# A hybrid decoder layer: four column groups for the sums of squares of q and k, and other orders at the ends of the feed-forwards

## The chip, the cores and the metric

The kernel runs on one core of one Trainium2 chip. The metric is the device time of one execution in microseconds (us), and less is better. Given are the median of three runs and one more execution that the hardware profiler recorded.

The engines are TensorE (PE; its weight loads are listed as PEld), VectorE (DVE), ScalarE (ACT), GpSimd (POOL) and SyncE (SP). Each works through its own instructions in a fixed order and stops at the first one whose operands are not there. SP, ACT and POOL also start DMA transfers, as instructions in that same order.

## What is computed

One layer of a decoder for 1024 prompt tokens and 8 sample tokens, so T = 1032 columns, with D = 1024 channels and FF = 2816:

```python
h = h + 0.5 * swiglu(rmsnorm(h, g1), w_gu1, w_down1)
u = rmsnorm(h, g) @ w_in           # q | k | v (512 each) | conv value, gate | pool input (256 each)
A = dilated_attention(qknorm(q), qknorm(k), v)      # 8 heads of 64
B = conv_module(glu(value, gate))  # depthwise conv, layernorm, swish, pointwise
C = causal_pooling(pool_input)
h = h + concat(A, B, C) @ w_out
h = h + 0.5 * swiglu(rmsnorm(h, g2), w_gu2, w_down2)
def swiglu(x, w_gu, w_down):
    g, u = split(x @ w_gu, 2)
    return (silu(g) * u) @ w_down
```

The new keys, values, conv and pool states are outputs too. All in float32.

## The kernel before, in words

Activations lie with channels on the 128 partitions and tokens in the free direction. The 1032 columns are two halves `HF` of 516, each two quarters of QT = 258; the mixer cuts them into three pieces `CH` of CW = 344. A float32 matrix product is done as three matmuls of high and low parts (hi\*hi, hi\*lo, lo\*hi): `hi` copies the high part on ACT (L241), `lo` subtracts it on DVE or POOL (L244).

The program's five stages are: feed-forward 1 (`up` and `down` with n = 1; up to about 700 us), the mixer with the input projection, attention, conv and pooling (to about 1080 us), `out_proj` (to about 1176 us), feed-forward 2 (`up` and `down` with n = 2).

**`up`** computes the gate and up products of 22 inner tiles f with a seven-product Strassen scheme. `product(f, i, ...)` is 24 matmuls of 128x258 (L512 to L514) into one of four double PSUM banks. Products 1 and 2 of a tile use the same bank, one after the other: ACT copies the first out (`v`, L521), then product 2 goes on in that bank. The first tiles do their products 1 and 2 early (`kept`, L522), while the norm of the input is still being made. `lag` sets by how many tiles product 2 is behind product 1 in the list `order` (L600 to L612): 1 in feed-forward 1, 3 in feed-forward 2 (L887). After the early ones each tile runs products 5, 7, 4, 3 of itself and 1, 2, 6 of a later one. Products 6, 7 and 4 of a tile go through one bank, one after the other, and product 4 waits until DVE has added product 7's state of it into `v` (L565).

The norm of feed-forward 1 (`norms`, L393 to L418): x is fetched (`fetch_x`, L380 to L383, DMA on POOL's queue), ACT squares it (L405), DVE adds up the eight squares of a half (L407), and `total` has PE sum over the partitions (L388), ACT take the root (`sd`, L390) and DVE the reciprocal (L391). It is done first for half 0, whose x are in place already, and then for half 1 (`x_287`, `x_289`, `x_291`, `x_293`, `x_339`, `x_341`, `x_343`, `x_345`). The weights `wr` come through SP's queue; `wop` are their high and low parts. Afterwards `mixed` (L420 to L460) normalizes x and makes the operands of the other products.

**`down`** (L763 to L815) runs seven passes over 11 inner tiles, the last being pass 3; at the end of a pass `add` (L777) puts the bank into `h` and `store` writes it out.

**The mixer** (L952 to L1185): for each of four pairs (q tile, k tile) and three pieces, ACT copies the projection out and squares it (`sq`), and a `total` (L1116 to L1119) sums the squares of the head channels with 32-column weights `sel` into `acc`, q into partitions 0 to 31 and k into 32 to 63. Then v is projected in groups of 24 matmuls of 128x256 (L1158 to L1160), each followed by a two-record matmul `mat,r` (L1164). Beside them, `side_v` (L1187 to L1225) makes the norm factors: for each piece DVE multiplies `acc` twice by r (L1198, L1199), ACT takes the root (L1200, with an activation table load first), DVE the reciprocal (L1201) and a product (L1202), then the high part goes to `rr` on ACT and the low part on DVE (L244). `norm(t)` (L1217) has PE spread `rr` over the partitions. `next(tail)` steps through `conv_tail`, the layernorm of the conv module: `sh` and `sl` (high on ACT, low on POOL) of the conv output `cy`, their mean over the channels by PE (L277, `ones`), its subtraction on DVE (L1305), then squares in the same way.

**`out_proj`** (L897 to L950) adds its 16 pieces into the residual, stores each to `hd2` (L934, POOL's queue) and squares it on ACT (L935). POOL adds up the squares for feed-forward 2.

A scheduler with a timeline of its own orders the instructions of each engine ahead of time, from the order and the priorities of the code; the engines then keep that order. So an edit in one place may also move other instructions.

## Time and profile before

| what | value |
|---|---|
| median of three runs | 1855.25 us (1853.35, 1855.25, 1856.14) |
| the profiled execution | 1856.26 us, of which its span is 1854.5 us |
| granted clock of PE over the span | 0.996 of full speed |
| busy in the span | PE 1822.7 us (98%), PEld 94%, DVE 72%, ACT 39%, POOL 12% |
| chain of work that ended last | PE 90%, DVE 4%, DMA 3%, ACT 2% |

PE works nearly all the time, so the time is PE's work plus the places where PE waits or runs at the lower clock. Those places are found in the view of PE's waits, and then looked at in the timeline. "[0.45 <-ACT v L521]" behind a row means that the engine was idle for 0.45 us and that ACT's instruction of line 521 on tile `v` released it.

### The profile page before, as it was taken

To read this page: it belongs to the slowest core of one execution; us is meant where nothing else is said; L and a number is where in the kernel's file an instruction comes from. 1 tells how busy PE (TensorE), PEld (TensorE's weight loads), DVE (VectorE), ACT (ScalarE), POOL (GpSimd) and SP (SyncE) were. 2 spreads that over 40 slices of the span, in tenths; PEclk is the share of its full clock that TensorE was granted. 3 is DMA by queue.
4 is the path that set the end of the run, shared out by engine and by line. 5 is a ranking of instruction groups with operands and counts; after the bars stand their busy time and mean duration, and the time that the engine had idled before them with its cause. 6 is when DMAs were issued, how large, how long until landed. Compare 5 with 4: busy or idle time off the path is not lost.

```text
span 1854.5 us, 35895 instructions
## 1 busy us (share of the span) xinstructions
PE 1822.7 (98%) x14436; PEld 1750.0 (94%) x14436; DVE 1343.4 (72%) x2140; ACT 724.7 (39%) x1307; POOL 213.4 (12%) x205
## 2 busy tenths in 40 slices
PE   7999999999999999999899999999999999999999
PEld 7999999999999999998865689989999999999999
DVE  6877787778686566997666755577777877868654
ACT  6532222322333455235655653443222222243342
POOL 2100000000000004732532423200000000000000
PEclk9999999999999999999999999999999999999999
DMA  9544365454964243212353256654433435596421
GB/s 330 195 139 149 115 182 191 144 183 161 327 244 118 84 158 94 53 38 75 121 159 115 93 170 207 216 169 158 131 127 111 142 120 181 168 325 245 117 81 46
DMA packets 155578, 286.72 MB, mean 155 GB/s; under 512 B 25992, under 2 KB 32732, under 8 KB 155412
## 3 DMA queue, kind: packets, MB, share of 16 engines
q1 hardware_dynamic: 116276, 206.21, 35.7%
q10 hardware_dynamic: 34560, 63.20, 9.1%
q0 software_dynamic: 4576, 15.01, 2.4%
q8 instruction: 113, 1.85, 0.4%
q14 instruction: 53, 0.43, 0.1%
HBM read 208.29 MB, written 78.61 MB: 155 GB/s over the span
## 4 chain that ended last, share of the span: by engine, by line
PE 90%; DVE 4%; DMA 3%; ACT 2%; issue 1%; SPq 0%; ACTq 0%; DVEq 0%
PE ps L512 15%; PE ps L513 15%; PE ps L514 15%; PE ps L773 8%; PE ps L774 8%; PE ps L775 8%; PE ps L283 5%; PE ps L284 5%; PE ps L285 5%; PE ps L1599 2%; PE ps L1580 1%; DMA wr<-wgu 1%; PE ps L1527 1%; DVE pt L1530 1%; PE ps L1528 1%; PE ps L1159 1%
## 5 line engine op out<-in xcount | busy, mean ns | idle before, releaser
L512 PE MATMUL ps<-xot,wop 128*128 128x258 f32 x1408 | 396.3, 283 | 1.8 <-DVE v L565 1.8
L513 PE MATMUL ps<-xot,wop 128*128 128x258 f32 x1408 | 397.9, 283 | 0.0
L514 PE MATMUL ps<-xot,wop 128*128 128x258 f32 x1408 | 397.0, 282 | 0.0
L773 PE MATMUL ps<-mop,wop 128*128 128x258 f32 x1232 | 348.1, 283 | 0.9 <-DVE v L578 0.9
L774 PE MATMUL ps<-mop,wop 128*128 128x258 f32 x1232 | 347.4, 282 | 0.0
L775 PE MATMUL ps<-mop,wop 128*128 128x258 f32 x1232 | 346.6, 282 | 0.0
L512 PE MATMUL ps<-xo,wop 128*128 128x258 f32 x1056 | 301.3, 286 | 6.1 <-ACT v L521 3.9
L513 PE MATMUL ps<-xo,wop 128*128 128x258 f32 x1056 | 300.0, 284 | 0.0
L514 PE MATMUL ps<-xo,wop 128*128 128x258 f32 x1056 | 299.6, 284 | 0.4 <-DVE wop L244 0.4
L512 PEld LDWEIGHTS ps<-xot,wop 128*128 128x128 f32 x1408 | 265.1, 189 | 2.9 <-issue 2.6
L513 PEld LDWEIGHTS ps<-xot,wop 128*128 128x128 f32 x1408 | 265.8, 189 | 1.5 <-issue 1.5
L514 PEld LDWEIGHTS ps<-xot,wop 128*128 128x128 f32 x1408 | 265.9, 189 | 0.0
L774 PEld LDWEIGHTS ps<-mop,wop 128*128 128x128 f32 x1232 | 233.5, 190 | 0.0
L773 PEld LDWEIGHTS ps<-mop,wop 128*128 128x128 f32 x1232 | 232.2, 189 | 1.1 <-issue 1.1
L775 PEld LDWEIGHTS ps<-mop,wop 128*128 128x128 f32 x1232 | 232.7, 189 | 0.0
L241 ACT ACTIVATE wop<-s 128x512 fp32r<-128x512 f32 x176 | 105.8, 628 | 292.6 <-DVE s L478 227.9
L512 PEld LDWEIGHTS ps<-xo,wop 128*128 128x128 f32 x1056 | 201.1, 191 | 9.0 <-ACT v L521 5.5
L514 PEld LDWEIGHTS ps<-xo,wop 128*128 128x128 f32 x1056 | 201.2, 191 | 0.9 <-DVE wop L244 0.8
L513 PEld LDWEIGHTS ps<-xo,wop 128*128 128x128 f32 x1056 | 201.4, 191 | 0.3 <-DVE xo L374 0.2
L244 DVE TENSOR_TENSOR wop<-wr,wop 128x512 fp32r<-128x512 f32 x180 | 121.7, 696 | 55.1 <-ACT wop L241 54.9
L244 DVE TENSOR_TENSOR wop<-s,wop 128x512 fp32r<-128x512 f32 x176 | 117.7, 688 | 36.1 <-ACT wop L241 35.6
L241 ACT ACTIVATE wop<-wr 128x512 fp32r<-128x512 f32 x180 | 107.2, 622 | 89.1 <-PE ps L775 76.7
(263 smaller groups left out, 3404.8 us busy)
## 6 DMA issues: line engine op xcount, KB each, us to landing
wr<-wgu SPq DMA_DIRECT2D x227, 256.0 KB
mt<-v ACTq DMA_DIRECT2D x88, 258.0 KB
mr<-mt SPq DMA_DIRECT2D x88, 258.0 KB
m<-v ACTq DMA_DIRECT2D x66, 258.0 KB
mr<-m SPq DMA_DIRECT2D x66, 258.0 KB
kept<-v ACTq DMA_DIRECT2D x52, 258.0 KB
v<-kept SPq DMA_DIRECT2D x52, 258.0 KB
h<-hd SPq DMA_DIRECT2D x48, 258.0 KB
```

The lines of the kernel that those rows point to most:

```text
L241: self.nc.scalar.activation(out, src, AF.Copy)
L244: (eng or self.nc.vector).tensor_tensor(out, src, hi.bitcast(F32), op=ALU.subtract)
L283: mm(out, wh, xh, start=i == 0, stop=False)
L284: mm(out, wh, xl, start=False, stop=False)
L285: mm(out, wl, xh, start=False, stop=i == n - 1)
L512: mm(out, wh, xh, start=start and k == 0, stop=False)
L513: mm(out, wh, xl, start=False, stop=False)
L514: mm(out, wl, xh, start=False, stop=stop and k == HK - 1)
L773: mm(out, wh, mh, start=opens, stop=False)
L774: mm(out, wh, ml, start=False, stop=False)
L775: mm(out, wl, mh, start=False, stop=closes)
L1599: mm(O[half[e], q1 - w:q1], vt[j // 2][:, j % 2, hc:hc + 64], pT[:, e, :], start=j == 0, stop=j == 2 * b + 1)
```

## The change

- `fetch_x` takes a queue, and the eight x of half 1 that `norms` fetches go through SP's queue instead of POOL's; those of `mixed` stay on POOL's.
- In the last inner tile of `up` product 7 comes ahead of product 5; the addition of product 5's bank (`add_c`) is then done after product 5.
- In pass 2 of `down` the four banks are taken at once; with n = 1 in the order 3, 0, 1, 2.
- In pass 3 of `down` the last of the four column pieces is done in two halves, each with its own addition (`add_half`).
- Feed-forward 2 gets lag 2 instead of 3.
- `out_proj` stores to `hd2` through ACT's queue instead of POOL's.
- The eight additions of `xs` (the sample tokens' x, 128x8 each) go from POOL to DVE.
- The sums of squares: a piece of 344 columns is cut into two of CH2 = 172, and `total` writes four groups of 32 partitions (q and k of the left, q and k of the right columns) with four matmuls of 172 columns instead of two of 344. Roots and reciprocals then take 128 partitions x 172 columns instead of 64 x 344; the products with r go by 64 partitions. The high part is first made in a tile `stath` and copied into `rr` in two parts.
- Between the factors and the first `norm`, `conv_tail` is advanced four times instead of two.

```diff
-        def fetch_x(k, hf):
+        def fetch_x(k, hf, queue=nc.gpsimd):
             x = tmp(f"x{hf}")
-            nc.gpsimd.dma_start(x, src(k, hf))
+            queue.dma_start(x, src(k, hf))
             return x
...
-            xs = [fetch_x(k, 1) for k in range(HK)]
+            xs = [fetch_x(k, 1, nc.sync) for k in range(HK)]
...
-                            xs += [fetch_x(i, 1) for i in range(HK, KT)]
+                            xs += [fetch_x(i, 1, nc.sync) for i in range(HK, KT)]
...
             val[f, "c"] = product(f, 5, "c", True, False)
+            if (f, 7) in val:
+                add_c(f)
...
-            nc.vector.tensor_tensor(two(v), two(v), val[f, "c"], op=ALU.add)
+            if (f, "c") in val:
+                add_c(f)
+
+        def add_c(f):
+            v = two(val[f, 7])
+            nc.vector.tensor_tensor(v, v, val[f, "c"], op=ALU.add)
...
-            order += [(5, f), (7, f)]
+            order += [(5, f), (7, f)] if i + 1 < NF else [(7, f), (5, f)]
...
-            if opens:
+            if opens and p == 2 and j == 0:
+                for b in (3, 0, 1, 2) if n == 1 else range(4):
+                    bank[b] = self.psp.tile([P, 2, 512], F32, tag="ps", name="ps")
+            elif opens and p != 2:
                 bank[j] = self.psp.tile([P, 2, 512], F32, tag="ps", name="ps")
...
-            for q in range(2):
+            for q in qs:
...
+        def add_half(j, q):
+            x = h[j][:, HT + q * QT:HT + (q + 1) * QT]
+            nc.vector.scalar_tensor_tensor(x, bank[j][:, q, 0:QT], 0.5, x, op0=ALU.mult, op1=ALU.add)
...
+                    if (p, j, b[-1]) == (3, 3, NP - 1):
+                        for q in range(2):
+                            for i in b:
+                                product(p, i, j, (q,))
+                            add_half(j, q)
+                        store(j, 1, h[j][:, HF[1]])
+                        continue
...
-                gen = self.up(lambda k, hf: hd2[k][:, HF[hf]], 2, "g2", False, 3)
+                gen = self.up(lambda k, hf: hd2[k][:, HF[hf]], 2, "g2", False, 2)
...
-            nc.gpsimd.dma_start(hd2[d][:, HF[hf]], x)
+            nc.scalar.dma_start(hd2[d][:, HF[hf]], x)
...
-                    for e in range(2):
-                        nc.tensor.matmul(acc[c][32 * e:32 * e + 32], sel[:, 32 * p:32 * p + 32], parts[e],
-                                         start=p == 0, stop=p == 3)
+                    for g in range(4):
+                        nc.tensor.matmul(acc[c][32 * g:32 * g + 32], sel[:, 32 * p:32 * p + 32],
+                                         parts[g % 2][:, g // 2 * CH2:(g // 2 + 1) * CH2],
+                                         start=p == 0, stop=p == 3, skip_group_check=True)
...
         for c in range(3):
-            r = self.r[0:64, CH[c]]
-            nc.vector.tensor_tensor(sc[c], acc[c][0:64], r, op=ALU.mult)
-            nc.vector.tensor_tensor(sc[c], sc[c], r, op=ALU.mult)
-            nc.scalar.activation(sc[c], sc[c], AF.Sqrt, bias=self.eps[0:64])
-            nc.vector.reciprocal(sc[c], sc[c])
-            nc.vector.tensor_tensor(sc[c], sc[c], r, op=ALU.mult)
+            x = sc[c][:, 0:CH2]
+            for h in range(2):
+                nc.vector.tensor_tensor(x[half[h]], acc[c][half[h]], self.r[half[h], cols(c, h)], op=ALU.mult)
+                nc.vector.tensor_tensor(x[half[h]], x[half[h]], self.r[half[h], cols(c, h)], op=ALU.mult)
+            nc.scalar.activation(x, x, AF.Sqrt, bias=self.eps)
+            nc.vector.reciprocal(x, x)
+            for h in range(2):
+                nc.vector.tensor_tensor(x[half[h]], x[half[h]], self.r[half[h], cols(c, h)], op=ALU.mult)
...
         for c in range(3):
-            self.hi(rr[0:64, CH[c]], sc[c])
-            self.lo(rr[64:128, CH[c]], sc[c], rr[0:64, CH[c]])
-        next(tail, None)
-        yield
-        next(tail, None)
-        yield
+            x, xh = sc[c][:, 0:CH2], self.t("stath", dt=F32R)[:, 0:CH2]
+            self.hi(xh, x)
+            for h in range(2):
+                nc.scalar.activation(rr[0:64, cols(c, h)], xh[half[h]].bitcast(F32), AF.Copy)
+                self.lo(rr[64:128, cols(c, h)], x[half[h]], xh[half[h]])
+        for _ in range(4):
+            next(tail, None)
+            yield
```

Three places show how the instructions stand. First ACT at the start of feed-forward 1. Before, from the table load for the root of half 0 to the root of half 1:

```order
L390 ACT_TABLE_LOAD
L390 ACTIVATE sd<-ps,eps 128x516
L241 ACTIVATE wop<-wr 128x512 x2
L522 DMA kept_3_161<-v_501 128x516
L405 ACTIVATE x_343<-x_343 128x516
L521 ACTIVATE v_539<-ps 128x516
L241 ACTIVATE wop<-wr 128x512
L405 ACTIVATE x_345<-x_345 128x516
L522 DMA kept_2_160<-v_539 128x516
L241 ACTIVATE wop<-wr 128x512
L390 ACTIVATE sd<-ps,eps 128x516
```

The same place on ACT after the change, from the copy of the sixth product to the root of half 0:

```order
L522 ACTIVATE v_501<-ps 128x516
L406 ACTIVATE x_345<-x_345 128x516
L523 DMA kept_0_158<-v_388 128x516
L242 ACTIVATE wop<-wr 128x512
L523 DMA kept_2_160<-v_428 128x516
L391 ACT_TABLE_LOAD
L391 ACTIVATE sd<-ps,eps 128x516
```

The last square of half 1 (`x_345`) stood behind the table load and the first root and now stands ahead of both. On DVE, in the same way, the sum that ends half 1 now stands ahead of the first reciprocal.

Second, ACT while v is projected. Before, from the first high part for the conv mean:

```order
L241 ACTIVATE sh_10176<-cy0_8947 128x344
L1165 ACTIVATE misc_8362<-ps_10114 128x1
L1200 ACT_TABLE_LOAD
L1200 ACTIVATE stat_10118<-stat_10118,eps_65 64x344
L241 ACTIVATE sh_10180<-cy1_9462 128x344
L1166 ACTIVATE v0_10030<-ps_10083,misc_8362 128x256
L241 ACTIVATE wboth_10138<-wr_10136 128x512
L1200 ACTIVATE stat_10119<-stat_10119,eps_65 64x344
L241 ACTIVATE sh_10213<-cy0_8947 128x344
```

After, from the first root to that same high part (`sh_10222`):

```order
L1229 ACTIVATE stat_10143<-stat_10143,eps_65 128x172
L1229 ACTIVATE stat_10144<-stat_10144,eps_65 128x172
L1229 ACTIVATE stat_10145<-stat_10145,eps_65 128x172
L1188 ACTIVATE misc_8363<-ps_10200 128x1
L1189 ACTIVATE v0_10049<-ps_10175,misc_8363 128x256
L1188 ACTIVATE misc_8363<-ps_10255 128x1
L1189 ACTIVATE v1_10050<-ps_10230,misc_8363 128x256
L242 ACTIVATE stath_10204<-stat_10143 128x172
L1240 ACTIVATE rr_10072<-stath_10204 64x172 x2
L242 ACTIVATE stath_10210<-stat_10144 128x172
L242 ACTIVATE stath_10216<-stat_10145 128x172
L242 ACTIVATE sh_10222<-cy0_8948 128x344
```

All six `sh` of the conv mean stood ahead of the second high part of the factors or among the roots; now the first stands behind the high parts of all three pieces, and the other five follow it. On PE the first matmul that reads `sh` comes after the third `mat,r` of the v groups in both; the first `norm` came after four v groups and comes after six now.

Third, PE among the early products of feed-forward 2. Before, where product 2 of a tile takes over the bank of product 1 (`ps_13945`):

```order
L512 MATMUL ps_13945<-xo11_13061,wop_13714 128x258
L513 MATMUL ps_13945<-xo11_13061,wop_13714 128x258
L514 MATMUL ps_13945<-xo11_13061,wop_13714 128x258
L513 MATMUL ps_13868<-xo21_13568,wop_13904 128x258
L514 MATMUL ps_13868<-xo21_13568,wop_13904 128x258
L512 MATMUL ps_13945<-xo21_13568,wop_13981 128x258
```

After, where product 1 of one tile ends and product 2 of an earlier tile begins:

```order
L513 MATMUL ps_14030<-xo11_13107,wop_13799 128x258
L514 MATMUL ps_14030<-xo11_13107,wop_13799 128x258
L515 MATMUL ps_14030<-xo11_13107,wop_13799 128x258
L513 MATMUL ps_13878<-xo21_13610,wop_13838 128x258
L514 MATMUL ps_13878<-xo21_13610,wop_13838 128x258
L515 MATMUL ps_13878<-xo21_13610,wop_13838 128x258
```

Before, two matmuls lay between the end of product 1 in a bank and the start of product 2 in it; now whole products of 24 matmuls lie between.

## Rows read from the trace of the kernel before

**Rows 1.** The view of waits of PE over the whole span: tile and line of the instruction that waited, what released it, us in total, how many times, the longest.

```profile
PE ps L388 <- DVE x L407: 5.7, 1, 5.7
PE ps L1217 <- DVE rr L244: 5.5, 3, 4.0
PE ps L512 <- ACT v L521: 3.9, 8, 0.7
PE ps L512 <- ACT wop L241: 2.2, 2, 1.3
PE ps L512 <- DVE v L565: 1.8, 2, 0.9
PE ps L388 <- ACT x L405: 1.5, 1, 1.5
PE ps L284 <- DVE xl L296: 1.3, 1, 1.3
```

**Rows 2.** The timeline of PE around the two totals of the norm in feed-forward 1: start in us, duration, engine, line, operation, names and shapes, count, idle time before it and what released it. Lines 388 are the totals, of half 0 and of half 1.

```profile
28.98 1.11 PE L388 MATMUL ps<-sq,mat 128*128 128x258 f32 x4 [1.49 <-ACT x L405]
29.74 0.47 PE L512 MATMUL ps<-xo,wop 128*128 128x258 f32 x1
35.56 0.28 PE L514 MATMUL ps<-xo,wop 128*128 128x258 f32 x1
41.58 2.06 PE L388 MATMUL ps<-x,mat 128*128 128x258 f32 x4 [5.74 <-DVE x L407]
43.08 0.78 PE L512 MATMUL ps<-xo,wop 128*128 128x258 f32 x1
47.16 0.28 PE L512 MATMUL ps<-xo,wop 128*128 128x258 f32 x1
```

**Rows 3.** The same stretch on ACT, DVE and POOL (timeline, as in rows 2): the last square of half 1, the reciprocal of half 0, the eighth fetch of x; from the view of DMA issues from 0 to 45 us the line of these fetches (count, KB each, median us from issue to landing); and from the view by stretches one of 2 us (length, then busy us and count on PE, PEld, DVE, ACT, POOL; granted clock of PE; DMA share; GB/s).

```profile
36.93 0.63 ACT L405 ACTIVATE x<-x 128x516 f32<-128x516 f32 x1
...
34.50 3.38 DVE L391 RECIPROCAL r<-sd 128x516 f32<-128x516 f32 x1 [1.23 <-ACT sd L390]
...
19.57 0.54 POOL L382 DMA_DIRECT2D x<-x  x1 [9.20 <-DVE sq L407]
...
x<-x POOLq DMA_DIRECT2D x15, 258.0 KB, 5.5
...
42.00:44.00 2.00, 2.00 (x7) 1.63 (x7) 0.00 (x0) 0.32 (x1) 0.33 (x2) 0.50 0.88 285
```

**Rows 4.** The timeline of PE at two of the eight waits among the early products of feed-forward 2.

```profile
1204.58 0.39 PE L512 MATMUL ps<-xo,wop 128*128 128x258 f32 x1 [0.45 <-ACT v L521]
...
1211.08 0.39 PE L512 MATMUL ps<-xo,wop 128*128 128x258 f32 x1 [0.45 <-ACT v L521]
```

**Rows 5.** The timeline of PE at the end of `up` and the start of `down` in feed-forward 1, and of DVE at the kernel's end.

```profile
463.97 0.36 PE L512 MATMUL ps<-xot,wop 128*128 128x258 f32 x1 [0.88 <-DVE v L565]
470.86 0.36 PE L773 MATMUL ps<-mop,wop 128*128 128x258 f32 x1 [0.88 <-DVE v L578]
...
1850.51 0.70 DVE L785 SCALAR_TENSOR_TENSOR h<-ps,h 128x516 f32<-128x516 f32 x1 [0.76 <-PE ps L775]
```

**Rows 6.** The chain of work that ended last, at the last store of `out_proj` (start, us, what), and the timeline of PE at the wait behind it.

```profile
1176.37 5.96 DMA hd<-h
...
1186.07 0.39 PE L512 MATMUL ps<-xo,wop 128*128 128x258 f32 x1 [0.94 <-ACT wop L241]
```

**Rows 7.** The timeline of PE and of its weight loads: one total of the sums of squares (L1118, two column groups) with the matmul after it, and the products of the sample tokens (L1075, four column groups of 32 partitions).

```profile
789.47 0.77 PE L1118 MATMUL ps<-sq,sel 128*32 128x344 f32 x4
790.17 0.43 PE L283 MATMUL ps<-xh,whi 128*128 128x344 f32 x1
...
865.73 1.05 PE L1075 MATMUL ps<-wr,xs 128*8 128x256 f32 x16
...
865.73 0.55 PEld L1075 LDWEIGHTS ps<-wr,xs 128*8 128x8 f32 x16 [0.21 <-issue]
```

**Rows 8.** The timeline of PE from the first conv mean (L277) past the first two norms (L1217); L1158 is a matmul of the v projection.

```profile
878.59 0.42 PE L277 MATMUL ps<-sh,ones 128*128 128x344 f32 x1
...
882.26 0.38 PE L1164 MATMUL ps<-mat,r 1*128 1x1 f32 x2
886.62 0.66 PE L1217 MATMUL ps<-rr,bcx 128*128 128x344 f32 x1 [3.98 <-DVE rr L244]
...
891.07 0.41 PE L1158 MATMUL ps<-whi,xh 128*128 128x256 f32 x1
893.56 0.28 PE L1158 MATMUL ps<-whi,xh 128*128 128x256 f32 x1
...
895.37 0.74 PE L1217 MATMUL ps<-rr,bcx 128*128 128x344 f32 x3
896.58 0.28 PE L1158 MATMUL ps<-whi,xh 128*128 128x256 f32 x1
```

**Rows 9.** The same stretch on ACT (the last copy of `bcx`, the table load for the roots) and on DVE (small additions, a reciprocal of one piece).

```profile
874.05 0.42 ACT L1192 ACTIVATE bcx<-bcr 128x256 fp32r<-128x256 f32 x1 [0.52 <-DMA bcr<-c_bc]
875.07 1.28 ACT L1200 ACT_TABLE_LOAD   x1
...
870.67 0.41 DVE L1084 TENSOR_TENSOR vs<-few 8x256 f32<-8x256 f32 x1
882.54 2.28 DVE L1201 RECIPROCAL stat<-stat 64x344 f32<-64x344 f32 x1
```

More of the change, by code (lines that the diff above doesn't have):

```diff
@@ L25 @@
 CW = T // 3
+CH2 = CW // 2
 CH = [slice(i * CW, (i + 1) * CW) for i in range(3)]
@@ L761, in down, with product @@
         mm = functools.partial(nc.tensor.matmul, skip_group_check=True)
-        def product(p, i, j):
+        def product(p, i, j, qs=(0, 1)):
             wt, mt = made[p, i]
             opens = p in (2, 4, 1, 5) and i == 0
-            if opens:
+            if opens and p == 2 and j == 0:
+                for b in (3, 0, 1, 2) if n == 1 else range(4):
+                    bank[b] = self.psp.tile([P, 2, 512], F32, tag="ps", name="ps")
+            elif opens and p != 2:
                 bank[j] = self.psp.tile([P, 2, 512], F32, tag="ps", name="ps")
@@ L1066, in mixer @@
         for k in range(KT):
-            nc.gpsimd.tensor_tensor(xs[:, k], self.xh[k][:, SEQ:T].bitcast(F32), self.xl[k][:, SEQ:T].bitcast(F32),
+            nc.vector.tensor_tensor(xs[:, k], self.xh[k][:, SEQ:T].bitcast(F32), self.xl[k][:, SEQ:T].bitcast(F32),
                                     op=ALU.add)
@@ L1085, in load_v @@
             return out
-        acc = [self.ps()[:, :CW] for _ in range(3)]
+        acc = [self.ps()[:, :CH2] for _ in range(3)]
         qk = [None] * 8
@@ L1194, in side_v, with cols @@
         yield
-        sc = [self.t("stat")[0:64] for _ in range(3)]
+        sc = [self.t("stat") for _ in range(3)]
+        half = [slice(0, 64), slice(64, 128)]
+        def cols(c, h):
+            return slice(c * CW + h * CH2, c * CW + (h + 1) * CH2)
         for c in range(3):
-            r = self.r[0:64, CH[c]]
-            nc.vector.tensor_tensor(sc[c], acc[c][0:64], r, op=ALU.mult)
-            nc.vector.tensor_tensor(sc[c], sc[c], r, op=ALU.mult)
-            nc.scalar.activation(sc[c], sc[c], AF.Sqrt, bias=self.eps[0:64])
-            nc.vector.reciprocal(sc[c], sc[c])
-            nc.vector.tensor_tensor(sc[c], sc[c], r, op=ALU.mult)
+            x = sc[c][:, 0:CH2]
[6 more added lines that the diff above has]
+                nc.vector.tensor_tensor(x[half[h]], x[half[h]], self.r[half[h], cols(c, h)], op=ALU.mult)
         tail = self.conv_tail()
```

## The prediction

> **What bounds the kernel now.** I read the view of PE's waits first [rows 1], because the page has PE busy 98% of the span: only where PE waits, or runs at the lower clock, is there anything to win. The seven lines are nearly all of it, and five of them lie where the change works: the totals of the first norm (L388), the norm factors of q and k (L1217), the early products of feed-forward 2 (L512 behind ACT's `v`), the last tile of each `up` (L565), and the operand behind the last store of `out_proj`. Then I went to the timeline of PE at each of them. There the reader is to see that the idle time shown understates the loss. After a wait the next matmuls start further apart. Between the two waits in [rows 4] lie 48 matmuls in 6.50 us. At the full pitch 48 take 5.8: in [rows 2] 48 stand between 29.74 and 35.56, 0.12 each. So 0.74 is lost where 0.45 is shown, and every short wait costs about 0.29 more than its idle time. After a long wait the clock is also lower: after the 5.74 us before the second total, PE's granted clock is 0.50 in the next stretch [rows 3], the 1.2 GHz level, and 18 matmuls take the 4.1 us from 43.08 to 47.16, 0.23 each [rows 2].
>
> **First norm: x on SP's queue.** In [rows 2] the second total starts at 41.58. Without a wait it would start at 35.68 (one pitch after 35.56), its first product 0.76 later as at the first total (28.98 to 29.74), and the 19th matmul of that product, which started at 47.16, at about 38.8. The loss is 47.16 - 38.8 = 8.4 us. What made it late is not the data. The eighth fetch was issued at 19.57 and such fetches land 5.5 us after issue [rows 3], so at about 25; ACT squared it at 36.93. Ahead of the square stood the table load and the root of half 0, and ahead of the sums on DVE the reciprocal of 3.38 us at 34.50 [rows 3]. With the change ACT's square stands ahead of the table load, right behind the copy of the sixth product, and the DVE sum ahead of the reciprocal. The sixth product's copy can follow PE's first total, about 29 to 30; with the copies, squares and operands queued on ACT there (0.5 us each) the last square ends at about 32.5 and the sum at 33.2, 2.4 us before PE wants it at 35.7. The eight fetches now queue behind nine loads of weights on SP and one of them behind a DVE sum; the last may land near 25 as before, so 7 us remain. I take the whole 8.3. If half the wait stays it is 4, which is the lower bound. The 1.49 us before the first total stay [rows 2]: about as many ACT instructions stand ahead of half 0's last square as before. The next work late could be `mixed`, which starts after the second reciprocal; that one moves forward by some 3.5 us where PE moves 8, and PE ran without a wait for 50 us behind it, so I put nothing there.
>
> **Last tile of `up`.** Product 4 waited 0.88 for DVE's L565 in both feed-forwards (1.8 in two, [rows 1]; one in [rows 5]). With product 5 between, 16 matmuls or 1.9 us lie over that 0.7 us addition. Gain (0.88 + 0.29) x 2 = 2.3. The added instruction order on DVE (`add_c` later) lies under product 4.
>
> **First banks of `down`.** The wait of 0.88 at 470.86 is for L578, which still reads a bank [rows 5]. Taking four banks at once in the order 3, 0, 1, 2 helps only if the first piece then gets a bank other than that one. By the order of allocation the first piece's bank is still the one of the last product 3. I take 0; it would be 1.2 if the banks do move.
>
> **Last piece in halves.** The end is one DVE addition of 0.70 after the last matmul [rows 5], then a store. Of two halves only the second stands there, about 0.43 (an estimate: half of the width, and a fixed part). Gain 0.3, once; in `down` 1 it is two rows for one on a DVE that does not bound PE there.
>
> **Lag 2.** Eight waits, each 0.74 by [rows 4], so 5.9 us. With the change 24 matmuls (2.9 us) lie between the two products in a bank where 2 lay, and the ACT copy takes 0.6. Feed-forward 1 has lag 1 in the same code, and no wait of this line appears there ([rows 1] has eight in all, which are those of feed-forward 2). I take 5.9; ACT being late at a few would leave 4.5.
>
> **`hd2` through ACT.** The wait at 1186.07 goes back to a store that took 5.96 us [rows 6]; the operand's page is free only then. On the other queue its issue is shorter by some 0.2 us, and the other transfers around it stay. I take 0.3, with 0 and 1.2 (0.94 + 0.29) as ends. **`xs` on DVE**: eight small additions, at most 0.41 each [rows 9], at a place where PE waits 1.3 us for DVE [rows 1]; they stand behind the operands it waits for, so 0, and up to 1 lost.
>
> **Sums of squares in four column groups.** A total of two groups keeps PE from 789.47 to 790.17, 0.70 us [rows 7]. There are 12. L1075 shows four groups: 16 records of 256 columns in about 1 us, with 16 weight loads that together take 0.55 [rows 7]. Per column and record that is 1.05 / (16 x 256), against 0.70 / (4 x 344) in the total, half as much; eight records of 172 columns are as many columns as four of 344. So 0.40 instead of 0.70, with some fixed part: gain 0.29 x 12 = 3.4. If only two groups ran side by side it would be about 0.70 and four more weight loads at 0.03 (0.55 / 16) each: a loss of 1.6 in all. The Trainium skill, "TensorE: Matmul & The Clock Gate", Part 3 on packing small matmuls, says that a weight load overlaps a running matmul only when the row group differs, which it does not here. By that the loads would stand between the matmuls and the gain shrink or turn; the trace does not agree, since in L1075 the row groups do not differ either and 16 loads and 16 matmuls fit into 1.05 us.
>
> **Norm factors.** Here I expect the wait to move, not to go. Before, the first norm waits at 886.62, and from 882.26 to 893.56 PE takes 11.3 us [rows 8]. At full speed that work (one `mat,r`, three norms and four conv means, which later take 1.21 from 895.37 to 896.58, and 12 matmuls of v) takes 2.9, so 8.4 are lost. The new chain is shorter: reciprocals of 172 columns at half of 2.28 [rows 9], so 3.4 less, and two more groups of v stand ahead of the first norm. `rr` is then ready some 8 us before PE comes. But the first conv mean on PE stands after the third `mat,r` as before, where PE comes at 878.59 less the three shortened totals, 877.7 [rows 8]. Its `sh` was on ACT ahead of the table load; now it stands behind the factors' high parts. The table load follows `bcx` at 874.05 and three small copies, about 875.6 [rows 9]; plus 1.28, a root of 0.4, three reciprocals of 1.14, two products on DVE of 0.3, then six ACT copies of under 0.42 [rows 9]: 883.5. So PE waits about 5.8 there, and such a wait cost 8.4 with its slow clock in [rows 2]. Net 0; I let it run from -3 to +4.
>
> **Sum.** 8.3 + 2.3 + 0 + 0.3 + 5.9 + 0.3 + 3.4 + 0 = 20.5. The profiled execution took 1856.26, so 1835.8; it lies 1.0 over the median, so 1834.8, say 1835.
>
> **Rivals.** (1) *The wait at the conv mean does not form*, because the factors' chain on ACT and DVE is done when PE comes. For it: the chain has 3.4 us less of reciprocals. Against: six high parts would have to come 6 us sooner than their rows give. Then the 8.4 go too: 1827. (2) *The second total is still late*: a fetch on SP that waits for a buffer lands after 33, and ACT, which keeps its order, stands before that square. For it: the fetches have 2 MB of weights ahead of them. Against: 7 us in hand. Then about 8 are not won: 1843. (3) *The column groups go two by two*: 5 us worse, 1840. L1075 speaks against it. The rule of the Trainium skill on weight loads, named above, would point the same way. (4) *Slower than before*: ACT's queue holds the stores of `out_proj`, and several of the 16 must first wait for an older DMA whose completion counter they take. Behind them on ACT stand the high parts of the next pieces' weights and the operands of feed-forward 2's first products. It decides where PE loses 1.3 us per store (16 x 1.3 = 20.5); if four stores held ACT for a landing like 5.96 [rows 6] and PE waited as long, 24 us would be lost, 1859. Against it: those DMAs were issued a piece or more before, over 5 us. (5) The banks of `down` do move: 1834; this is inside my own range.
>
> **How the numbers follow.** Forecast 0.67, (1) 0.14, (2) 0.10, (3) 0.05, (4) 0.04. The forecast's own range is 1830 to 1841: the norm factors by -3 to +4, the early products by 1.4, the first norm by 2, the totals by 1, the store by 0.9. With (1), and (2) as the upper end, 1827 to 1843 leaves out under 2 in 10. A measurement of this kernel can tell 0.2% or 3.7 us from no change. All but (4) are faster by more than that: faster 0.94, same 0.03, slower 0.03.
>
> **What would show it.** No wait over 1 us before the second L388, and a granted clock of 1.0 from 30 to 60 us; the wait at the first L388 still there. No L512 behind ACT's `v` after 1200, none behind L565. The wait before `down`'s first matmul still there. A total of the sums of squares in about 0.4 us. No wait of the norms for `rr`, but one of 4 to 7 us of the first conv mean for ACT's `sh`, near 860 to 870 in the new times, with a slow clock behind it. I am wrong if PE waits for x there longer than 3 us, or not at all at the conv mean, or anywhere in `out_proj`.

## The result and the profile after

| | before | after |
|---|---|---|
| time, median of 4 runs each, us | 1855.7 (1853.35 to 1856.7) | 1837.16 (1835.65 to 1842.49) |
| profiled execution, us | 1856.26 | 1842.49 |
| span in that profile, us | 1854.5 | 1840.7 |
| PE busy | 98% | 99% |

The changed kernel takes 0.9907 of the time before (95% interval 0.9885 to 0.9929): 18.5 us less. The profiled execution of after is the slowest of its four runs. The lines of code stand lower now: 388 is L389, 512 is L513, 565 is L568, 773 is L784, 1118 is L1140, 277 is L278.

The view of PE's waits after the change (columns as in [rows 1]):

```profile
PE ps L278 <- ACT sh L242: 6.2, 1, 6.2
PE ps L513 <- DVE v L568: 4.1, 4, 2.2
PE ps L784 <- DVE h L790: 2.5, 2, 2.0
PE ps L784 <- DVE v L586: 0.9, 1, 0.9
PE ps L513 <- DVE h L955: 0.5, 1, 0.5
```

The first three lines of [rows 1] are gone: the second total's 5.7, the norms' 5.5, the 3.9 of the early products. One long wait took the norms' place, at the first conv mean (L278). Two entries grew where the prediction had them shrink or did not have them: L568 (1.8 before, 4.1 now), and L790, the addition of half a piece (2.5).

**The two totals.** Timeline of PE, and the view by stretches from 40 to 60 us (columns as in [rows 3]):

```profile
26.74 1.03 PE L389 MATMUL ps<-sq,mat 128*128 128x258 f32 x4
...
33.11 1.03 PE L389 MATMUL ps<-x,mat 128*128 128x258 f32 x4
```

```profile
40.00:60.00 20.00, 20.00 (x170) 20.00 (x169) 19.96 (x32) 12.63 (x23) 2.61 (x5) 1.00 0.93 316
```

Beside [rows 2]: neither total has an idle time before it, the second starts at 33.11 instead of 41.58, and the clock stays at 2.4 GHz (granted 1.00), where one of the stretches before had 0.50 [rows 3].

**A total of the sums of squares.** Timeline of PE and its weight loads, after; beside [rows 7]:

```profile
785.72 0.50 PE L1140 MATMUL ps<-sq,sel 128*32 128x172 f32 x8
786.15 0.43 PE L284 MATMUL ps<-xh,whi 128*128 128x344 f32 x1
...
785.72 0.16 PEld L1140 LDWEIGHTS ps<-sq,sel 128*32 128x32 f32 x8 [0.21 <-issue]
```

Each of these matmuls stands as two records in the trace. Eight records (four matmuls) now take 0.43 us (785.72 to 786.15) where four records (two matmuls) took 0.70. Eight records of weight loads lie inside it.

**The norm factors.** Timeline of ACT and DVE up to the first `sh`, then of PE from the third `mat,r` on:

```profile
869.93 1.28 ACT L1229 ACT_TABLE_LOAD   x1
871.22 1.10 ACT L1229 ACTIVATE stat<-stat,eps 128x172 f32<-128x172 f32 x3
...
875.66 0.35 ACT L242 ACTIVATE stath<-stat 128x172 fp32r<-128x172 f32 x1 [2.21 <-DVE stat L1232]
876.03 0.70 ACT L1240 ACTIVATE rr<-stath 64x172 fp32r<-64x172 f32 x2
876.76 0.66 ACT L242 ACTIVATE stath<-stat 128x172 fp32r<-128x172 f32 x2
877.33 0.47 ACT L242 ACTIVATE sh<-cy 128x344 fp32r<-128x344 f32 x1
...
871.69 3.40 DVE L1230 RECIPROCAL stat<-stat 128x172 f32<-128x172 f32 x3 [1.56 <-ACT stat L1229]
```

```profile
871.27 0.38 PE L1187 MATMUL ps<-mat,r 1*128 1x1 f32 x2
877.85 0.66 PE L278 MATMUL ps<-sh,ones 128*128 128x344 f32 x1 [6.21 <-ACT sh L242]
878.31 0.41 PE L1181 MATMUL ps<-whi,xh 128*128 128x256 f32 x1
878.52 0.42 PE L1182 MATMUL ps<-wlo,xh 128*128 128x256 f32 x1
```

The reader is to see the queue: three roots, three reciprocals, the high parts of all pieces, and only then `sh`, for which PE has stood since 871.6. Behind the wait the matmuls of v start 0.21 apart instead of 0.12: half speed, until 882.8.

**The last piece in halves.** Timeline of PE and of DVE at the end of `down` 1, and two stretches (columns as in [rows 3]):

```profile
685.64 0.28 PE L786 MATMUL ps<-mop,wop 128*128 128x258 f32 x1
687.90 0.39 PE L784 MATMUL ps<-mop,wop 128*128 128x258 f32 x1 [1.98 <-DVE h L790]
...
689.09 0.49 PE L284 MATMUL ps<-xh,whi 128*128 128x344 f32 x1
...
685.69 0.69 DVE L800 SCALAR_TENSOR_TENSOR h<-ps,h 128x516 f32<-128x516 f32 x1
686.30 1.22 DVE L245 TENSOR_TENSOR wlo<-wr,whi 128x1024 fp32r<-128x1024 f32 x1
687.43 0.42 DVE L790 SCALAR_TENSOR_TENSOR h<-ps,h 128x258 f32<-128x258 f32 x1
```

```profile
686.00:688.00 2.00, 0.10 (x1) 0.10 (x1) 2.00 (x4) 2.00 (x4) 0.00 (x0) 1.00 0.40 151
688.00:690.00 2.00, 2.00 (x10) 2.00 (x11) 2.00 (x4) 2.00 (x4) 0.00 (x0) 0.56 0.65 162
```

The products of the second half go into the same double bank as those of the first, and the first of them starts when DVE's addition of the first half (L790, 687.43) is over. DVE had another addition and a 1.22 us low part ahead of it. Then the granted clock is 0.56, and 0.58 in the next 2 us: the 1.2 GHz level for most of both.

**The last tile of `up` in feed-forward 1.** ACT's store of a tile `v`, DVE and PE:

```profile
448.47 0.33 ACTq L605 DMA_DIRECT2D m<-v  x1
...
454.93 0.70 DVE L591 TENSOR_TENSOR v<-v,v 128x516 f32<-128x516 f32 x1 [2.84 <-DMA m<-v]
455.54 0.69 DVE L568 TENSOR_TENSOR v<-ps,v 128x516 f32<-128x516 f32 x1
...
456.38 0.55 PE L513 MATMUL ps<-xot,wop 128*128 128x258 f32 x1 [2.21 <-DVE v L568]
...
464.66 0.36 PE L784 MATMUL ps<-mop,wop 128*128 128x258 f32 x1 [0.88 <-DVE v L586]
```

DVE stands at L591, which writes over a tile that the store still reads; L568, for which PE waits, is queued behind it. The last row is the wait before `down`, 0.88 as in [rows 5].

### The profile page after: what moved, and what is told of

The parts are those of the page before. It is cut to its first block, busy times and chain, and to the rows that moved or that the text cites. A ratio compares the mean times of both kernels' runs of the same rounds, so it can differ in the third digit from the quotient of the medians.

```text
span 1840.7 us, 35978 instructions
## 1 busy us (share of the span) xinstructions
PE 1816.3 (99%) x14484; PEld 1749.6 (95%) x14484; DVE 1341.9 (73%) x2162; ACT 725.5 (39%) x1313; POOL 191.7 (10%) x173
## 4 chain that ended last, share of the span: by engine, by line
PE 92%; DVE 3%; DMA 2%; ACT 1%; issue 1%; SPq 0%; DVEq 0%; ACTq 0%
PE ps L513 15%; PE ps L514 15%; PE ps L515 15%; PE ps L784 8%; PE ps L786 8%; PE ps L785 8%; PE ps L284 5%; PE ps L285 5%; PE ps L286 5%; PE ps L1631 2%; PE ps L1612 1%; PE ps L1559 1%; DVE pt L1562 1%; DMA m<-v 1%; PE ps L1560 1%; PE ps L1182 1%
## 5 line engine op out<-in xcount | busy, mean ns | idle before, releaser
L513 PE MATMUL ps<-xot,wop 128*128 128x258 f32 x1408 | 396.7, 284 | 4.1 <-DVE v L568 4.1
L784 PE MATMUL ps<-mop,wop 128*128 128x258 f32 x1232 | 348.1, 283 | 3.4 <-DVE h L790 2.5
L513 PE MATMUL ps<-xo,wop 128*128 128x258 f32 x1056 | 300.0, 284 | 2.0 <-ACT wop L242 1.5
L513 PEld LDWEIGHTS ps<-xot,wop 128*128 128x128 f32 x1408 | 265.6, 189 | 5.4 <-issue 3.4
L784 PEld LDWEIGHTS ps<-mop,wop 128*128 128x128 f32 x1232 | 232.3, 189 | 4.0 <-DVE h L790 2.9
L513 PEld LDWEIGHTS ps<-xo,wop 128*128 128x128 f32 x1056 | 200.0, 189 | 3.3 <-ACT wop L242 2.2
```

Of the source, the lines that this page charges most:

```text
L513: mm(out, wh, xh, start=start and k == 0, stop=False)
L784: mm(out, wh, mh, start=opens, stop=False)
```

## Experiments

Times are medians, each against the kernel before as it was measured beside it (1855.2 us for e1 to e4, 1855.03 for e5 to e8). A ratio comes with its 95% interval.

**e1: the changed kernel again**, unedited.

> The changed kernel unchanged, once more. Theory: the four waits of the last products of the first up for DVE (4.1 us in all, the longest 2.2) belong to that one execution, which took 1842.49 where the median is 1837.2; they go back to single transfers that landed late (6.4 us), so another profile shows them elsewhere or shorter, while the 6.2 us at the conv mean and the 2.0 us at the end of the first down stand at the same places with the same lengths within 0.3. Rival: they come with the change, because TensorE reaches those products 8 us earlier than before and the transfers do not; then they come back at the same places with 3 to 5 us in sum. Time 1836 to 1838 in either case.

Measured: 1838.89 us (1837.29 to 1841.2), ratio 0.9917 (0.9902 to 0.9931). The waits at `sh` (6.38), at L790 (1.97 and 0.52), at the last tile's L568 (1.98) and before `down` (0.87) come again. The waits for L568 at 413 and 428 us in the profile above (0.30 and 1.30) do not come again here, nor in e2 and e3; waits of that addition of 0.31 to 1.25 us stand near there in e4, e5 and e6. So those two come and go between executions, while the longest one, which my theory gave to that execution as well, comes with the change.

**e2: no halves.**

```
-                    if (p, j, b[-1]) == (3, 3, NP - 1):
-                        for q in range(2):
-                            for i in b:
-                                product(p, i, j, (q,))
-                            add_half(j, q)
-                        store(j, 1, h[j][:, HF[1]])
-                        continue
```

> The change without the halves of the last piece of down (both feed-forwards). Theory: the second half waits for the first half's addition, 2.0 us plus a stretch at the lower clock in feed-forward 1 and 0.5 plus the refill at the kernel's end; without it both waits go and the time falls by 3 to 5 us against the changed kernel, to 1832 to 1834. Rival: in feed-forward 1 the wait only goes back to the mixer's first operand, as in the kernel before (1.3 us for xl), and at the end the halves do save 0.3; then the time falls by less than 2 us.

Measured: 1834.56 us (1834.09 to 1835.57), ratio 0.9893 (0.9878 to 0.9908), 4.3 us less than e1. Both waits for L790 are gone. In the profiles, from `down`'s first product to the first conv mean it is 409.31 us (460.92 to 870.23), in e1 413.39 (461.99 to 875.38): 4.1 of it is there. At the very end, from the start of the last but one piece's addition to the end of the last, e2 takes 2.12 us and after 2.65 (DVE at the end of e2, then of after):

```profile
1827.24 0.70 DVE L800 SCALAR_TENSOR_TENSOR h<-ps,h 128x516 f32<-128x516 f32 x1 [0.75 <-PE ps L786]
1828.66 0.70 DVE L800 SCALAR_TENSOR_TENSOR h<-ps,h 128x516 f32<-128x516 f32 x1 [0.72 <-PE ps L786]
```

```profile
1834.77 0.69 DVE L800 SCALAR_TENSOR_TENSOR h<-ps,h 128x516 f32<-128x516 f32 x1 [0.72 <-PE ps L786]
1835.48 0.43 DVE L790 SCALAR_TENSOR_TENSOR h<-ps,h 128x258 f32<-128x258 f32 x1
1836.99 0.43 DVE L790 SCALAR_TENSOR_TENSOR h<-ps,h 128x258 f32<-128x258 f32 x1 [1.08 <-PE ps L786]
```

So the halves lose at both places. The last addition is shorter (0.43 for 0.70), but PE stands 0.52 for the first one.

**e3: `sh` ahead of the factors' high parts.** All three pieces of the conv tail are split at once, and that step is called ahead of the factors.

```
         tail = self.conv_tail()
         next(tail, None)
+        next(tail, None)
         yield
...
-            if c < 3:
-                split(c, [y[t][:, CH[c]] for t in range(2)])
+            if c == 0:
+                for i in range(3):
+                    split(i, [y[t][:, CH[i]] for t in range(2)])
```

> The change with the high and low parts for the conv mean (all three pieces) written ahead of the factors' high parts, their sums by TensorE behind as they were. Theory: the 6.2 us wait of the first conv mean is only the place of sh behind the factors on ScalarE; with sh ahead it falls under 2 us, the clock stays up and the time falls by 5 to 8 us, to 1829 to 1832. Rival: the chain of roots and reciprocals then reaches rr too late and the norm waits for it, as before the change, with 4 us or more; the time stays within 2 us of 1837.

Measured: 1831.79 us (1828.34 to 1833.25), ratio 0.9875 (0.986 to 0.9889), 7.1 less than e1. ACT makes the first three `sh` ahead of the table load, and PE takes the conv mean without a wait, although it now comes to it one group of v earlier, behind the second `mat,r` (ACT, PE, and the stretch, of e3):

```profile
861.75 0.48 ACT L242 ACTIVATE sh<-cy 128x344 fp32r<-128x344 f32 x1
...
865.64 1.28 ACT L1229 ACT_TABLE_LOAD   x1
...
863.50 0.43 PE L278 MATMUL ps<-sh,ones 128*128 128x344 f32 x1
...
879.53 0.74 PE L1250 MATMUL ps<-rr,bcx 128*128 128x344 f32 x3
```

```profile
860.00:880.00 20.00, 19.86 (x147) 18.62 (x148) 15.55 (x36) 14.74 (x42) 11.69 (x13) 1.00 0.23 75
```

The last `rr` of e3 is written on DVE by 877.2, and PE comes to the first norm at 879.53. So the factors are no bound any more; the place of `sh` on ACT was.

**e4: lag 2 alone**, in the kernel before.

```
-                gen = self.up(lambda k, hf: hd2[k][:, HF[hf]], 2, "g2", False, 3)
+                gen = self.up(lambda k, hf: hd2[k][:, HF[hf]], 2, "g2", False, 2)
```

> The kernel before with lag 2 instead of 3 in feed-forward 2 and nothing else. Theory: each of the eight waits costs 0.74 us from start to start, so 5.9 us in all: ratio 0.9968, about 1849.8, and no wait for the copy of product 1. Rival: a wait costs only its idle time, 3.9 us in all, 1851.8; or the schedule elsewhere moves and gives part of it back.

Measured: 1849.48 us (1848.66 to 1850.96), ratio 0.9971 (0.996 to 0.9983), 5.7 less. No wait for ACT's `v` is left. Eight waits with an idle time of 3.9 in all were worth 5.7. The interval of the ratio (3.2 to 7.4 us) does not exclude the rival's 3.9 by itself; the profiles do. From the wait behind `out_proj` to `down`'s first product in feed-forward 2 it is 442.31 us before (1186.07 to 1628.38) and 436.42 in e4 (1185.44 to 1621.86): 5.9 less. So these short waits cost more than the idle time that is shown.

**e5: x on SP alone**, in the kernel before.

```
-            xs = [fetch_x(k, 1) for k in range(HK)]
+            xs = [fetch_x(k, 1, nc.sync) for k in range(HK)]
...
-                            xs += [fetch_x(i, 1) for i in range(HK, KT)]
+                            xs += [fetch_x(i, 1, nc.sync) for i in range(HK, KT)]
```

> The kernel before, with the 16 fetches of x for half 1 of the first norm on SP's queue and nothing else. My theory: both totals of the first norm lose their wait by this alone, the second its 5.7 us and the slow clock behind it (8.3 us in all), the first its 1.5 us, which I had said would stay: about 10 us off, a ratio near 0.9946. Rival: the first total's wait went through another part of the change; then it is still there and 8.3 us come off, a ratio near 0.9955. Second rival: PE that comes earlier at the end of up only waits there instead; then the L565 wait of feed-forward 1 grows from 0.9 to over 2 us and less than 8 us come off.

Measured: 1844.19 us (1843.87 to 1846.49), ratio 0.9939 (0.9922 to 0.9955), 10.8 less. Neither total waits. `down`'s first product comes at 460.60, 10.3 before the 470.86 of [rows 5]. So the first total's 1.49 went through this part too. (Eight fetches move in this edit; the 16 of my expectation is wrong.)

What I had not seen is why. Before, seven of these fetches are issued on POOL from 6.67 us on, while the weights are being loaded through SP's queue, and ACT stands for three weights `wr` in a row, 1.15 us up to 12.65 and then twice 1.23 (the first two rows). In e5 the seven are issued on SP at 13.91, behind nine loads of weights, and ACT waits for no weight (ACT before; SP and ACT of e5, with the first squares):

```profile
14.52 0.63 ACT L241 ACTIVATE wop<-wr 128x512 fp32r<-128x512 f32 x1 [1.23 <-DMA wr<-wgu]
16.38 0.63 ACT L241 ACTIVATE wop<-wr 128x512 fp32r<-128x512 f32 x1 [1.23 <-DMA wr<-wgu]
...
13.91 3.75 SPq L382 DMA_DIRECT2D x<-x  x7
...
15.52 2.19 ACT L405 ACTIVATE sq<-x 128x516 f32<-128x516 f32 x4
```

The first square of half 0 starts at 17.39 before and at 15.52 here. The three waits stand in all three kernels with x on POOL (before, e4, e8), and in none of the seven with x on SP. So the queue did two things: it moved the squares to another place in ACT's order, as predicted, and it let the weights land first.

The last tile's wait stays at 0.88 (453.71); another L565, at 427.37, waited 1.25.

**e6: the last tile in the old order**, in the changed kernel.

```
-            order += [(5, f), (7, f)] if i + 1 < NF else [(7, f), (5, f)]
+            order += [(5, f), (7, f)]
```

> The changed kernel with the last inner tile in the old order, product 5 before product 7, in both feed-forwards. My theory: the wait of 2 us that PE has for L568 in feed-forward 1 comes from DVE, which stands at L591 for a store that lands 6 us after its issue, and L568 is queued behind it; with the old order the wait is then still 1.5 to 2.2 us there, and only feed-forward 2 gets its 0.9 us back: about 1 us slower than the changed kernel. Rival: the new order itself makes the wait, since product 7's addition now comes 3 us sooner into DVE's queue; then both waits are 0.9 us with the old order, and the time is the same or 1 us better. The waits tell it, the times hardly.

Measured: 1836.85 us (1836.49 to 1837.6), ratio 0.99 (0.9886 to 0.9915): no slower than the changed kernel. My theory missed. (The times compare more than this edit: e6's profile has waits of 1.27 us at the first total, for a copy `v` on ACT, and of 0.89 for `xl` at the mixer, which after and e1 do not have, and no slow clock behind its wait for L790, which they have.) In feed-forward 2 the last tile's wait is back at 0.88. With the old order the wait in feed-forward 1 is 0.88, not 1.5 to 2.2 (ACT, DVE and PE of e6, the rows that answer to those of after):

```profile
447.04 0.33 ACTq L605 DMA_DIRECT2D m<-v  x1
...
451.74 0.69 DVE L591 TENSOR_TENSOR v<-v,v 128x516 f32<-128x516 f32 x1 [1.09 <-DMA m<-v]
452.99 0.69 DVE L568 TENSOR_TENSOR v<-ps,v 128x516 f32<-128x516 f32 x1 [0.55 <-PE ps L515]
...
453.83 0.36 PE L513 MATMUL ps<-xot,wop 128*128 128x258 f32 x1 [0.88 <-DVE v L568]
```

Two things differ. L568 follows product 7, which stands last here, so DVE waits for PE again (0.55) and the store is hidden. And the store itself lands sooner: from its issue to L591's start it is 4.70 us here and 6.46 in after. In all kernels with the old order it is 4.7 to 5.2 (before, e4, e5, e6, e8), in all with the new one 5.5 to 6.5 (after, e1, e2, e3). The issues on SP, ACT and POOL stand in the same order and at nearly the same distances in both: in after and in e6 SP issues six loads between 0.6 us before the store and 2.2 us behind it, and the DMA share is 0.84 to 1.10 from 1 us after the store's issue until it lands. Why the store is slower with the new order stays open.

**e7: three mends**, in the changed kernel: those of e2 and e3, and a tile of its own for the difference of L591.

```
-                rest.append(lambda: mix("t1", m, u, m))
-                val["pair"] = u, m
+                d = tmp("vd")
+                rest.append(lambda: mix("t1", d, u, m))
+                val["pair"] = u, d
```

> The changed kernel with three mends: the last piece of down not in halves, the conv tail's operands sh all made ahead of the high parts of the norm factors, and the difference t1 of L591 written into a tile of its own instead of the one that a store still reads. My theory: 4 us from the first, 7 from the second (both as measured alone), 2 to 3 from the third, since the wait of about 2 us for L568 and the slow clock behind it go: 1823 to 1825, a ratio near 0.983. Rival: the third brings nothing, because L568 then waits for something else on DVE or ACT (the extra tile takes a buffer that a later store still reads): 1827.

Measured: 1822.58 us (1821.33 to 1823.18), ratio 0.9822 (0.9807 to 0.9837). All that is left of PE's waits in e7:

```profile
PE ps L1627 <- DVE pT L1615: 1.7, 4, 0.6
PE ps L513 <- ACT wop L242: 1.5, 1, 1.5
PE ps L653 <- DVE eps L876: 1.2, 1, 1.2
PE ps L1608 <- DVE st L1558: 0.6, 1, 0.6
PE ps L1428 <- DVE kt L1415: 0.6, 1, 0.6
PE ps L514 <- DVE xo L375: 0.2, 1, 0.2
```

No wait for L568 is left, and that of 0.88 before `down` went too, which I had not expected: in e7 PE starts `down` at 457.83, before the addition that it waited for elsewhere (L586, at 458.03), so that product must have another bank; I did not follow why. With the 4.3 and 7.1 of e2 and e3, the 1838.89 of e1 becomes 1827.5; the other 4.9 came with the third mend, if the gains add. e1's own runs lie 3.9 us apart, so the profiles are the better measure: from the second total to `down`'s first product it is 424.91 us in e7 (32.92 to 457.83) and 427.28 to 429.57 in e1, e2 and e3, so 2.4 to 4.7 less. I had given it 2 to 3; about 1.2 of it is the wait before `down` (0.88 and, by estimate, 0.29 more). It was not run alone.

**e8: four column groups alone**, with the norm factors and the conv tail's order behind them, in the kernel before. Its main lines:

```
-        acc = [self.ps()[:, :CW] for _ in range(3)]
+        acc = [self.ps()[:, :CH2] for _ in range(3)]
...
-                    for e in range(2):
+                    for g in range(4):
...
-        sc = [self.t("stat")[0:64] for _ in range(3)]
+        sc = [self.t("stat") for _ in range(3)]
```

> The kernel before with the four column groups of the sums of squares alone: the totals, the norm factors on 128 partitions and the order of the conv tail behind them, nothing at the feed-forwards. My theory: 12 totals at 0.3 us less each, 3.3 us, and the norms' wait of 5.5 us turned into one of about 6 us of the first conv mean for sh, which costs as much: 1852, a ratio near 0.998. Rival: the norm factors' part costs or gains something of its own as well: over 1855 (nothing gained), or under 1849.

Measured: 1851.92 us (1849.61 to 1853.35), ratio 0.9983 (0.9973 to 0.9992), 3.1 less. PE's only wait in this stage (e8):

```profile
880.44 0.65 PE L278 MATMUL ps<-sh,ones 128*128 128x344 f32 x1 [5.95 <-ACT sh L242]
```

So the totals gain about 3 us and the wait of the norms becomes one of the conv mean at about the same price; the time shows the two together only (1.5 to 5.0 us less by its interval).

## Why the prediction held, and which terms did not

The time fell near the forecast, and the three large terms have in the main the mechanism that the prediction gave them. Of the small ones, one came to nothing and one had the wrong sign; the first norm, which gave 2.5 more than its term, covers part of that. So it is in part luck that the sum came out so near: 20.5 forecast, 18.5 and 16.3 measured.

| step of the prediction | forecast, us | measured, us | from |
|---|---|---|---|
| first norm: x on SP | 8.3 | 10.8 | e5 |
| lag 2 | 5.9 | 5.7 | e4 |
| sums of squares and norm factors | 3.4 and 0 | 3.1 together | e8 |
| last tile of `up` | 2.3 | about 0, or a small loss | after and e1 against e6 |
| last piece in halves | 0.3 | -4.3 | e1 against e2 |
| first banks of `down` | 0 | wait unchanged (0.88) | after |
| `hd2` through ACT | 0.3 | not told apart | after and e8 |

The measured ones add up to 15.3; after and e1 lie 18.5 and 16.3 under the kernel before as measured beside them. By their intervals the first norm gave 8.3 to 14.5, lag 2 3.2 to 7.4, the sums of squares 1.5 to 5.0. Terms of a few us cannot be added more closely than that.

- **First norm.** The order on ACT and DVE is as predicted. The step that failed is that the first total's 1.49 "stay", and "What made it late is not the data" holds for x alone: ACT had stood 3.6 us for weights before its squares (see e5). I had counted ACT's instructions ahead of half 0's last square, not when they can start. In after the first square starts at 15.90 (17.39 before), ACT's last square of half 0 stands at 24.23 now and stood at 26.77; half 1's last at 28.77, which I had ending at about 32.5. The first total's wait is gone in six of the seven profiles with x on SP; in e6 ACT waits 1.20 us for DVE among the squares (21.84), and that total waits 1.27. The rival of a late second total did not occur.
- **Lag 2.** Right, and with it the price of 0.74 for an idle time of 0.45.
- **Sums of squares.** 0.27 less per total against 0.29. The rival of groups two by two fell: eight loads and eight matmuls fit into 0.43. The Trainium skill, "TensorE: Matmul & The Clock Gate", Part 3, lets a weight load overlap a running matmul only for another row group; as in [rows 7] the trace does not agree, since the row groups are the same here.
- **Norm factors.** Right as forecast: no wait for `rr`, but 6.21 (5.8 forecast) of the conv mean for `sh`, with half the clock behind it, and nothing gained. e3 shows the cause: with `sh` moved ahead, the wait goes and 7.1 us with it. The rival without this wait (1827) did not occur.
- **Last piece in halves.** The step that failed reads "in `down` 1 it is two rows for one on a DVE that does not bound PE there". DVE does bound PE there, since splitting makes the second half's products wait for the first half's addition. I costed the addition that got shorter, and not the wait that the split adds between its halves. 1.98 of idle time and a slow clock at one place, 0.52 at the other. The two halves are different columns of the bank; that they wait for each other because they share one tile is argued, since no run gave each half a tile of its own.
- **Last tile.** "16 matmuls or 1.9 us lie over that 0.7 us addition" holds in feed-forward 2, where 0.88 became 0.29 (product 5 has 24 matmuls, 2.9 us, as the prediction itself counts a product under lag 2). In feed-forward 1 I left out what stands ahead of the addition on DVE: L591, which waits for a store. The old order hid that wait behind product 5; the new one puts the addition, and so PE, behind it. The trace of before had it: DVE stood 1.20 us for the same store there (L583 at 461.99), unseen by PE.
- **`hd2` through ACT.** Forecast 0.3. The wait of 0.94 at the end of `out_proj` is gone in after, and one of 0.52 for L955 stands near it. e8, which keeps the old queue, has the same 0.52. So I cannot give the queue any of it. The rival that it makes the kernel slower did not occur.
- **`xs` on DVE.** Forecast 0. The 1.32 that PE waited for `xl` before the mixer (699.22 before) stands in e4 and e8 too, is 0.71 in e5 and 0.89 in e6, and gone in e2 and e7. No run has this edit alone, so what it did is not shown.

Not settled: why the store of the last tile lands later with the new order, and what each of the third mend's effects in e7 is worth alone.

## What to carry to other kernels

Splitting the last piece of work in two pays only if the second part does not wait for what follows the first: here, with both halves in one PSUM tile, the reader of the first half stood between PE and the second. A fetch that is not needed yet can hold up one that is: with eight fetches of x behind the weights on one queue, ACT no longer stood for weights, its squares moved, and 10 us came off. Before moving a product so that its addition comes sooner, look at what that addition is queued behind; a wait that is hidden today may be next in line. And where a wait moves from one operand to another, the cheapest edit is often the order on the engine that makes both: here a few small instructions ahead of a chain of roots and reciprocals were worth 7 us.

## What the runs showed of the hardware

- A wait of PE of about 2 us was followed by some 3 us at the 1.2 GHz level in some executions and by none in others. Behind the 1.97 to 1.98 us for L790 in `down` 1 the clock fell in after (granted 0.56 and 0.58 in two stretches of 2 us), e1 (0.50 from 687 to 689) and e3 (0.50 from 685 to 687), and stayed at 1.00 in e6. At the last tile of `up` 1 it fell after 2.21 us (after, matmuls 0.21 apart for about 3 us) and 1.98 (e1), and stayed at 1.00 after 2.03 (e2) and 1.30 (e3). Behind the waits of 5.7 to 6.4 us at the totals and the conv mean it was at 1.2 GHz every time. Where it fell, 2 us of idle time cost close to 4 (e2 against e1).
- A store of 258 KB took 4.7 to 6.5 us from its issue to the instruction that it held up, at the same place of the program. DVE came to that instruction 3.6 to 3.8 us after the issue, so it stood for 1.1 to 2.8 us.
- Seven fetches of 258 KB issued on POOL's queue beside the loads of weights went with three waits of ACT for weights of 0.79 to 1.25 us each; issued on SP behind nine of these loads, with none (before, e4, e8 against the seven others).
- Eight matmul records of 172 columns on 32 output partitions each, in four column groups, took 0.43 us, four of 344 in two groups 0.70.
